# The w_out sums and parts on VectorE and ScalarE, in 44 held steps

## The chip, the cores and the metric

The kernel runs on one core of a Trainium2 chip. The metric is the device time of one execution in microseconds (us). Engines are named as in the profile: PE is TensorE, DVE VectorE, ACT ScalarE, POOL GpSimd; SP is the engine that issues the DMAs.

## The reference

One step of a streaming encoder layer: 4096 prompt frames and 64 sample frames of width 1024. A projection feeds two groups of heads with gated linear recurrences, each branch has a SiLU gate, and an output projection closes the layer. What matters here is the end:

```python
    o_a = rms_norm(o_a, g_on_gla).reshape(B, T, GLA_V) * jax.nn.silu(z_a)
    o_h = rms_norm(o_h, g_on_hgrn).reshape(B, T, HGRN_W) * jax.nn.silu(z_h)
    o = jnp.einsum('bte,ed->btd', jnp.concatenate([o_a, o_h], axis=-1), w_out)
    y = x + gate[:, None] * rms_norm(o, g_post)
```

`z_h` is the last of the input projections; the line with `z_h` is the gate part, the einsum with `w_out` the output product.

## The kernel before

The program runs in stages: setup and first group, the GLA projections and recurrence in 16 groups of 256 frames, the HGRN projections and recurrence in 16 groups, the gate part, and the output product. All float32 products are made from two parts: a high part `hi` (a cast to the matmul's format, on ScalarE) and a low part `lo` (source minus `hi`). Three matmuls, hi by hi, hi by lo, lo by hi, make one product. The helper `split` (L87 to L94) makes both parts: the cast is L93, the subtraction L94, on VectorE unless another engine is handed in.

**The gate part** is `zrun` in `run`. It goes through 33 tiles: two of 128 frames for each of the 16 groups, and the 64 sample frames as a third tile of group 2. For each group, `split_h` makes the parts `hh` of the normalised input in four pieces (casts on ScalarE, subtractions on VectorE), `hh` has five buffers, and `load_hf` starts the loads of the next group's input. `z_tile` (L1240 to L1256) loads one tile of `oh`, makes 24 matmuls of 128x512 (eight k, three products each, L624), a sigmoid on ScalarE (L1252), two products on VectorE (L1253, L1254) and stores the tile. A tile gives three yields: after half of its matmuls, at its end, and once in `zrun`.

**The output product** (`project`) multiplies two-by-two blocks with seven products in place of eight. It needs seven weight forms per k tile: B11, B21, B22 as they are, and the sums T1 to T4. **`load_wout`** (L1267) makes them from `w_out`: in each of four rounds (`kt`) it loads two pieces of 128x1024 (L1284) into the two buffers of the staging pool, scales each by a column of norm gains on ScalarE (L1285), makes four sums in place (L1290) and splits seven blocks of 128x512 into hi and lo (`put`). A staging buffer is loaded again for the next round when its last reader is done. The seven results go to the rooms `wv`, `wb` and `wc`.

**The order.** `weave(main, sides)` runs a main generator and, between its steps, so many steps of each side generator. The tuple `(generator, n, first, last)` spreads n side steps evenly over the main steps from `first` to `last`. What comes out is a program order. A scheduler then orders each engine's queue by simulated readiness, so an instruction whose inputs are ready early may go ahead of others traced before it; the engine itself takes its queue in order. `keep_in_program_order(ins)` ties an instruction behind the one traced just before it on the same engine: an edge of issue order only, which does not wait for that instruction to finish. Instructions traced later are not tied by it.

The last tiles of the gate part are run after the weave, the last one inside `project`. The gate part from tile 8 to tile 29 is the main of the weave at L1672: 22 tiles, 66 main steps. Its only side is `load_wout`, in 16 steps over main steps 0 to 56.

Of the kernel before, what the change touches and what calls it, by code (L numbers as in the profile page):

```python
# [6 lines left out]
F32 = mybir.dt.float32  # L7
# [3 lines left out]
AF = mybir.ActivationFunctionType  # L11
ALU = mybir.AluOpType
# [16 lines left out]
class Kernel:  # L29
# [1108 lines left out]
    def attend_group(self, g, S, Ss, res, G, NS, scratch, out_p, out_s):  # L1138
# [4 lines left out]
        def run(i):  # L1143
# [28 lines left out]
            )  # L1172

        main = run(0)
        if len(sets) == 1:
            yield from main
        else:

            sample = run(1)
            level = None  # L1180
            for _ in main:
                if level is not LEVELS:
                    level = next(sample)
                    if level is LEVELS:
                        nc.sync.dma_start(self.s_room, self.state_ap(Ss[0], G, NS))
                        Ss[0] = self.s_room
                yield
            assert level is LEVELS
            yield from sample
            nc.sync.dma_start(self.state_ap(out_s, G, NS), Ss[0])  # L1190
# [76 lines left out]
    def load_wout(self, room):  # L1267

        nc = self.nc
        W = self.W3  # L1270
        names = ("B11", "B21", "B22", "T1", "T2", "T3", "T4")
        for n in names:
            W[n] = []
        rooms = [("wv", i) for i in range(8)] + [("wb", i) for i in range(8)]

        def unit():
            u = self.wunit(rooms.pop(0)[0]) if rooms else room.tile([P, 1024], F32R, name="wc", bufs=12)
            return u[:, :1024].rearrange("p (two c) -> p two c", two=2)

        def load(kt):  # L1280
            sts = []
            for q in range(2):
                st = self.stage_pair()[:, :D]
                nc.sync.dma_start(st, self.t["w_out"][0, (4 * q + kt) * P : (4 * q + kt + 1) * P, :])  # L1284
                nc.scalar.activation(st, st, AF.Copy, scale=self.col[:, 50 + q : 51 + q])  # L1285
                sts += [st[:, :512], st[:, 512:]]
            return sts

        def sub(dst, a, b):
            nc.gpsimd.tensor_tensor(dst, a, b, ALU.subtract)  # L1290

        for kt in range(4):
            b11, b12, b21, b22 = load(kt)
            yield
            us = {n: unit() for n in names}

            def put(n, src):
                self.split(us[n][:, 0], us[n][:, 1], src, nc.gpsimd)


            put("B11", b11)
            sub(b11, b12, b11)
            sub(b12, b22, b12)
            yield
            put("B22", b22)
            put("B21", b21)
            sub(b22, b22, b11)
            sub(b21, b21, b22)
            yield
            for n, src in (("T1", b11), ("T3", b12), ("T2", b22), ("T4", b21)):  # L1310
                put(n, src)
            for n in names:
                W[n].append(us[n])
            yield
# [267 lines left out]
    def run(self):  # L1582
        nc, t = self.nc, self.t
        self.W1 = W1 = {"qk": [], "z": [], "v": []}
        self.W2 = W2 = {"q": [], "f": [], "i": []}
        self.W3 = W3 = {"z": [], "o": []}

        def now(gen):
            for _ in gen:
                pass  # L1590

        self.setup()
        ng = self.ng
        with ExitStack() as rec:
            self.open_recurrence(rec)
            self.setup_late()
            for i in range(4):
                nc.sync.dma_start(self.h_d[0][:, 2 * i : 2 * i + 2, :], self.hf[i])
            h = lambda k: self.h0[k // 2][:, :, k % 2]
            S, Ss = [None], [t["state_gla"]]  # L1600
            side = None

            def prep_x(g):
                if g > 1:
                    self.x_load(g, [0, 1])
                (self.x_norm if g < 2 else self.quad_norm)(g, [0, 1])
                for _ in range(3):
                    yield
                yield from self.x_turn(g)

            def prep_h(g, tl):
                self.load_hf(g, tl)
                yield

            for g in range(ng):
                prep = prep_x(g + 1) if g + 1 < ng else prep_h(0, self.groups2[0])
                sides = [(side, 12, 1, 18), (prep, 8, 0, 16) if g == 0 else (prep, 8, 7, 19)]
                if g == ng - 1:

                    sides.append((self.weights(W2["f"], C_FH, 512, "wa"), 10, 8, 18))  # L1620
                    sides.append((self.weights(W2["q"], C_QH, 512, "wv"), 10, 20, 26))
                res = self.weave(self.proj_gla(g, h), sides)
                h = self.split_h()
                side = self.attend_group(g, S, Ss, res, 2, 2, self.oa_d, t["new_gla_p"], t["new_gla_s"])
                next(side)
            S, Ss = [None], [t["state_hgrn"]]
            gate = self.gate_rows()
            per_gate = -(-28 // max(1, ng - self.beside - 2))
            for g in range(ng):
                prep = prep_h(g + 1, self.groups2[g + 1]) if g + 1 < ng else prep_h(0, self.groups2[0])  # L1630
                sides = [
                    (side, 15 if g == 0 else 16 if g == self.beside + 1 else 12, 1, 18), (prep, 1, 4, 8),
                    (gate if g > self.beside + 1 else None, per_gate, 0, END),
                ]
                if g == 0:
                    sides.append((self.weights(W2["i"], C_IH, 512, "wb"), 10, 0, 14))
                if g == ng - 1:
                    sides.append((self.weights(W3["z"], C_ZH, 512, "wa"), 10, 8, 18))
                res = self.weave(self.proj_hgrn(g, h), sides)
                h = self.split_h()  # L1640
                side = self.attend_group(g, S, Ss, res, 4, 1, self.oh_d, t["new_hgrn_p"], t["new_hgrn_s"])
                next(side)
            now(gate)
            tiles = [(g, j, tl) for g in range(ng) for j, tl in enumerate(self.groups2[g])]
            self.done = 0

            def zrun():
                hh = h
                for i, (g, j, tl) in enumerate(tiles):
                    if j == 0 and i > 0:  # L1650
                        hh = self.split_h()
                        if len(self.groups2[g]) == 3:
                            self.pair_up(hh, [self.stage_pair(F32R)])
                    if j == 0 and g + 1 < ng:
                        self.load_hf(g + 1, self.groups2[g + 1])
                    yield from self.z_tile(hh, tiles[i])
                    self.done += 1
                    yield

            zg = zrun()  # L1660

            def until(n):
                while self.done < n:
                    next(zg)
                    yield

            self.weave(until(8), [(side, 15, 0, 22)])
        self.x_room.close()
        with ExitStack() as s:
            room = self.pool(s, "w3", reuse_waits="tile")  # L1670
            self.ogp = self.pool(s, "og", reuse_waits="tile")
            self.weave(until(len(tiles) - 3), [(self.load_wout(room), 16, 0, 56)])  # L1672
            ogs = [self.og_half(0, j, q, self.ep if j else None) for j in range(2) for q in range(2)]
            now(until(len(tiles) - 1))
            self.project(ogs, lambda: now(zg))
# [58 lines left out]
```

## Time and profile before

| what | value |
|---|---|
| time, median of 3 runs | 2133.59 us (2131.57 to 2134.98) |
| the profiled execution's own time | 2135.26 us |
| its span, first to last instruction | 2133.4 us |
| granted TensorE clock, mean | 0.991 |

The page's second part cuts the span into 40 slices of 53 us; the gate part lies in slices 29 to 33, counted from 0. The digits are busy tenths.

```profile
DVE  6877776777767778687888788777786446777775
ACT  5666655666555655445444444444444434333432
POOL 3200011000010111110000001100125502232321
PEclk9999999999999999999999999999999899999999
```

GpSimd's two fives are slices 30 and 31, the one 8 of the clock is slice 31, VectorE's two fours are slices 31 and 32.

In the rows that follow, a timeline row has the start, the duration, the engine, the line, the operation, out<-in, shape and count, and in brackets the idle time ahead of it and what ended it. Matmuls are pipelined, so a row's duration is a merged one and its end is modelled. DMA waits are put down to the transfer that landed last.

### The profile page before, as it was taken

The numbers are of one execution on the slowest core, as the hardware profiler recorded it, in microseconds if no ns is written. First come the engines' busy times: TensorE is split into PE (matmuls) and PEld (weight loads), VectorE is DVE, ScalarE is ACT, GpSimd is POOL, SyncE is SP. The second block draws the span as 40 slices with busy tenths as digits, with TensorE's granted clock in tenths as the row PEclk, the third lists the DMA queues.
The fourth block names the chain that finished last, engine by engine and source line by source line (L and its number), as shares of the span: only waits on it lengthen the run. The fifth ranks groups of instructions, "written<-read, shape, count | busy, mean of one in ns | idle before, by whom it ended". The sixth has DMA issues, their size and how long they took to land.

```text
span 2133.4 us, 45130 instructions
## 1 busy us (share of the span) xinstructions
PE 2073.7 (97%) x16390; PEld 1817.6 (85%) x16390; DVE 1563.9 (73%) x4742; ACT 1061.4 (50%) x3124; POOL 376.2 (18%) x745
## 2 busy tenths in 40 slices
PE   7999999999999999999999999999999799999998
PEld 5888898988988888989988989999876688888886
DVE  6877776777767778687888788777786446777775
ACT  5666655666555655445444444444444434333432
POOL 3200011000010111110000001100125502232321
PEclk9999999999999999999999999999999899999999
DMA  8422222222222331011111101110245565354442
GB/s 253 122 56 73 67 59 53 55 67 67 58 56 51 104 114 43 31 36 58 50 51 60 52 31 36 31 31 31 75 149 179 171 197 163 131 166 138 158 143 95
DMA packets 236106, 190.00 MB, mean 89 GB/s; under 512 B 138220, under 2 KB 160208, under 8 KB 235884
## 3 DMA queue, kind: packets, MB, share of 16 engines
q1 hardware_dynamic: 235740, 186.86, 29.5%
q8 instruction: 129, 2.11, 0.4%
q14 instruction: 93, 0.76, 0.1%
q10 hardware_dynamic: 144, 0.26, 0.0%
HBM read 126.60 MB, written 60.45 MB: 88 GB/s over the span
## 4 chain that ended last, share of the span: by engine, by line
PE 80%; DVE 9%; ACT 4%; POOL 2%; DMA 2%; issue 2%; SPq 1%; DVEq 0%; ACTq 0%; POOLq 0%
PE ps_pj L624 28%; PE ps_pj L612 21%; PE ps_pj L1336 12%; PE ps_ms L844 2%; PE ps_o L828 2%; PE ps_o L823 2%; PE ps_o L1336 2%; PE ps_at L691 2%; PE ps_at L963 2%; DVE wst L914 2%; PE ps_at L771 1%; PE ps_tp L798 1%; POOL wst L1290 1%; DMA wst<-in_w_in_dram 1%; ACT A L781 1%
## 5 line engine op out<-in xcount | busy, mean ns | idle before, releaser
L612 PE MATMUL ps_pj<-hh,wa 128*128 128x256 f32 (+1 forms) x2976 | 392.1, 287 | 0.0
L624 PE MATMUL ps_pj<-wb,hh 128*128 128x512 f32 x1536 | 378.8, 396 | 0.9 <-ACT K L1043 0.9
L612 PEld LDWEIGHTS ps_pj<-hh,wa 128*128 128x128 f32 x2976 | 372.7, 191 | 4.9 <-issue 0.3
L624 PEld LDWEIGHTS ps_pj<-wb,hh 128*128 128x128 f32 x1536 | 280.3, 188 | 59.1 <-issue 2.7
L612 PE MATMUL ps_pj<-hh,wv 128*128 128x256 f32 (+1 forms) x1536 | 213.2, 289 | 0.0
L624 PE MATMUL ps_pj<-wa,hh 128*128 128x512 f32 x768 | 190.1, 406 | 16.1 <-ACT hh L93 8.7
L612 PEld LDWEIGHTS ps_pj<-hh,wv 128*128 128x128 f32 x1536 | 191.8, 188 | 12.1 <-issue 9.3
L624 PE MATMUL ps_pj<-wv,hh 128*128 128x264 f32 x1464 | 199.3, 290 | 1.6 <-DVE wv L94 1.6
L624 PEld LDWEIGHTS ps_pj<-wa,hh 128*128 128x128 f32 x768 | 147.2, 195 | 53.9 <-ACT hh L93 11.8
L624 PEld LDWEIGHTS ps_pj<-wv,hh 128*128 128x128 f32 x1464 | 184.1, 188 | 6.8 <-issue 2.3
L945 POOL COPY T<-T 128x16 f32<-128x16 f32 (+1 forms) x32 | 9.9, 310 | 1007.6 <-DVE Qg L884 904.3
L94 DVE TENSOR_TENSOR hh<-hf,hh 128x512 fp32r<-128x512 f32 (+1 forms) x188 | 140.5, 756 | 41.9 <-ACT hh L93 40.9
L1208 ACT ACTIVATE g<-ps_pj 128x256 f32<-128x256 f32 (+1 forms) x128 | 49.6, 387 | 228.2 <-PE ps_pj L612 227.6
L93 ACT CAST hh<-hf 128x512 fp32r<-128x512 f32 (+1 forms) x188 | 116.9, 624 | 68.6 <-PE ps_pj L624 52.8
L914 DVE TENSOR_TENSOR wst<-wst,T 128x160 f32<-128x160 f32 (+4 forms) x480 | 108.5, 266 | 1.1
L1396 ACT ACTIVATE sq<-e 128x512 bf16<-128x512 f32 x64 | 40.4, 631 | 119.1 <-DVE e L1408 116.1
L1336 PE MATMUL ps_pj<-wc,wa 128*128 128x512 f32 x384 | 98.3, 391 | 0.0
L1399 POOL TENSOR_TENSOR e<-e,gg 128x512 f32<-128x512 f32 x32 | 41.4, 1293 | 294.5 <-ACT sq L1396 178.5
L938 ACT ACTIVATE A<-Ac,member 128x128 f32<-128x128 f32 x256 | 80.8, 390 | 24.4 <-DVE Ac L932 24.4
L947 POOL TENSOR_TENSOR T<-T,T 128x16 f32<-128x16 f32 (+1 forms) x224 | 83.8, 374 | 17.0
L1336 PEld LDWEIGHTS ps_pj<-wc,wa 128*128 128x128 f32 x384 | 72.0, 188 | 16.0
L932 DVE COPY_PREDICATED Ac<-mask,ps_at 128x112 f32<-128x112 uint8 (+6 forms) x448 | 77.4, 224 | 1.0 <-PE ps_at L963 0.9
(337 smaller groups left out, 4082.2 us busy)
## 6 DMA issues: line engine op xcount, KB each, us to landing
hf<-h_d SPq DMA_DIRECT2D x128, 256.0 KB
h_d<-hf SPq DMA_DIRECT2D x64, 256.0 KB
oh_d<-e SPq DMA_DIRECT2D x64, 256.0 KB
xq<-in_x_prompt_dram SPq DMA_DIRECT2D x64, 256.0 KB
out_y_prompt_dram<-xq SPq DMA_DIRECT2D x63, 256.0 KB
xt<-in_x_prompt_dram SPq DMA_DIRECT2D x448, 32.0 KB
wst<-in_w_in_dram SPq DMA_DIRECT2D x36, 256.0 KB
e<-oh_d SPq DMA_DIRECT2D x33, 256.0 KB
```

The lines of the kernel that those rows point to most:

```text
L93: self.nc.scalar.copy(hi, src)
L94: (eng or self.nc.vector).tensor_tensor(lo, src, hi.bitcast(F32), ALU.subtract)
L612: self.nc.tensor.matmul(ps[:, :T], a, b, start=i == 0, stop=i == n - 1)
L624: self.nc.tensor.matmul(ps[:r, : c1 - c0], a, b, start=kt == 0 and i == 0, stop=kt == KT - 1 and i == 2)
L691: nc.tensor.transpose(pt[:, i * P : (i + 1) * P], D[:, c + i, :], self.ident)
L823: nc.tensor.matmul(po[h], A[:, c * 4 + h, :], v, start=h < n, stop=St is None and h == 4 - n)
L914: nc.vector.tensor_tensor(parts(dst), parts(src), t.unsqueeze(3).to_broadcast(shape), ALU.mult)
L932: nc.vector.copy_predicated(Ach[:, :, 4 * a :].rearrange("p h (j m) -> p h j m", m=4), self.mask[:CL, : 8 - a].unsqueeze(1).unsqueeze(3).t ...
L938: nc.scalar.activation(Ah[:, :, 32 * b : 32 * b + 32], Ach, AF.Copy, scale=self.member[:CL, 8 + b : 9 + b])
L947: nc.gpsimd.tensor_tensor(E8[:, :, i], E8[:, :, i - 1], T8[:, :, i], ALU.mult)
L1208: nc.scalar.activation(sg, pf[:, :T], AF.Sigmoid)
L1336: nc.tensor.matmul(bank, u[:, a, kt, :], W[name][kt][:, b], start=kt + i == 0, stop=kt + i == 5)
```

## The change

`load_wout` is rewritten in its order and its engines. The four sums (`sub`) and the low parts (in `put`) are computed by VectorE where GpSimd computed them. Loads and scalings are separated: the scalings follow two yields after the loads, with a yield after each. Each round has 11 yields where it had four, with at most one `put` and one sum between two of them; the seven puts come in another order. Each scaling, cast, sum and low part is tied by `keep_in_program_order`; the loads are not. The weave spreads 44 steps over main steps 0 to 62.

```diff
+        here = self.tc.keep_in_program_order
+
+        def sub(dst, a, b):
+            here(nc.vector.tensor_tensor(dst, a, b, ALU.subtract))
+
         def load(kt):
             sts = []
             for q in range(2):
                 st = self.stage_pair()[:, :D]
                 nc.sync.dma_start(st, self.t["w_out"][0, (4 * q + kt) * P : (4 * q + kt + 1) * P, :])
-                nc.scalar.activation(st, st, AF.Copy, scale=self.col[:, 50 + q : 51 + q])
-                sts += [st[:, :512], st[:, 512:]]
+                sts.append(st)
             return sts
 
-        def sub(dst, a, b):
-            nc.gpsimd.tensor_tensor(dst, a, b, ALU.subtract)
-
         for kt in range(4):
-            b11, b12, b21, b22 = load(kt)
-            yield
+            sts = load(kt)
+            yield
+            yield
+            for q, st in enumerate(sts):
+                here(nc.scalar.activation(st, st, AF.Copy, scale=self.col[:, 50 + q : 51 + q]))
+                yield
+            b11, b12, b21, b22 = [st[:, o : o + 512] for st in sts for o in (0, 512)]
             us = {n: unit() for n in names}
 
             def put(n, src):
-                self.split(us[n][:, 0], us[n][:, 1], src, nc.gpsimd)
+                here(nc.scalar.copy(us[n][:, 0], src))
+                sub(us[n][:, 1], src, us[n][:, 0].bitcast(F32))
 
 
             put("B11", b11)
+            yield
             sub(b11, b12, b11)
+            put("B22", b22)
+            yield
             sub(b12, b22, b12)
-            yield
-            put("B22", b22)
+            put("T1", b11)
+            yield
+            sub(b22, b22, b11)
+            put("T3", b12)
+            yield
             put("B21", b21)
-            sub(b22, b22, b11)
+            yield
             sub(b21, b21, b22)
-            yield
-            for n, src in (("T1", b11), ("T3", b12), ("T2", b22), ("T4", b21)):
-                put(n, src)
+            put("T2", b22)
+            yield
+            put("T4", b21)
             for n in names:
                 W[n].append(us[n])
             yield
...
-            self.weave(until(len(tiles) - 3), [(self.load_wout(room), 16, 0, 56)])
+            self.weave(until(len(tiles) - 3), [(self.load_wout(room), 44, 0, 62)])
```

## The prediction

> **What bounds the kernel now.** I read the page first, then the same views cut down to the stage that the change touches. The page gives one row for TensorE as a whole and one for the gate part's matmuls (out<-in, shape, count, busy us, mean ns, then the idle time ahead of them and what ended it).
>
> ```profile
> PE 2073.7 (97%) x16390; PEld 1817.6 (85%) x16390; DVE 1563.9 (73%) x4742; ACT 1061.4 (50%) x3124; POOL 376.2 (18%) x745
> L624 PE MATMUL ps_pj<-wa,hh 128*128 128x512 f32 x768 | 190.1, 406 | 16.1 <-ACT hh L93 8.7
> ```
>
> TensorE is busy 97% of the span, so only its idle time and its slow time can be won. The gate matmuls have 16.1 us of idle ahead of them, more than half of it ended by the cast of the next `hh` on ScalarE. Cutting the stage into stretches shows where (busy us and counts by engine, granted clock, DMA):
>
> ```profile
> core 0: us, PE busy (x) PEld busy (x) DVE busy (x) ACT busy (x) POOL busy (x), PEclk, DMA share, GB/s
> 1561.00:1606.50 45.50, 45.50 (x326) 35.24 (x325) 40.77 (x128) 23.06 (x58) 10.78 (x26) 1.00 0.52 165
> ...
> 1615.00:1636.00 21.00, 19.08 (x74) 14.32 (x72) 11.92 (x11) 9.17 (x16) 14.87 (x11) 0.92 0.52 175
> 1636.00:1650.00 14.00, 11.32 (x46) 8.40 (x46) 8.95 (x8) 6.22 (x12) 12.51 (x8) 1.00 0.43 136
> 1650.00:1670.00 20.00, 13.64 (x44) 9.60 (x44) 7.78 (x8) 7.96 (x14) 14.87 (x11) 0.77 0.49 165
> 1670.00:1688.60 18.60, 13.51 (x48) 10.22 (x48) 9.11 (x10) 11.21 (x19) 15.47 (x11) 0.87 0.50 157
> 1688.60:1770.00 81.40, 81.38 (x353) 67.22 (x354) 39.94 (x60) 24.52 (x41) 0.00 (x0) 0.98 0.60 191
> ```
>
> From 1615 to 1688.6 GpSimd is busy three quarters of the time, and TensorE has gaps and a granted clock down to 0.77. From 1688.6, when GpSimd has nothing left, TensorE has no gap. In order of time, TensorE's rows are:
>
> ```profile
> 1606.52 13.77 PE L624 MATMUL ps_pj<-wa,hh 128*128 128x512 f32 x60
> 1620.79 0.73 PE L624 MATMUL ps_pj<-wa,hh 128*128 128x512 f32 x2 [0.50 <-ACT hh L93]
> 1622.65 13.11 PE L624 MATMUL ps_pj<-wa,hh 128*128 128x512 f32 x48 [1.13 <-DVE hh L94]
> 1636.49 10.16 PE L624 MATMUL ps_pj<-wa,hh 128*128 128x512 f32 x42 [0.73 <-DVE hh L94]
> 1647.50 1.20 PE L624 MATMUL ps_pj<-wa,hh 128*128 128x512 f32 x4 [0.85 <-DVE hh L94]
> 1650.31 2.80 PE L624 MATMUL ps_pj<-wa,hh 128*128 128x512 f32 x6 [1.61 <-ACT hh L93]
> 1654.03 10.11 PE L624 MATMUL ps_pj<-wa,hh 128*128 128x512 f32 x36 [0.91 <-ACT hh L93]
> 1667.18 0.73 PE L624 MATMUL ps_pj<-wa,hh 128*128 128x512 f32 x2 [3.04 <-ACT hh L93]
> 1670.20 12.78 PE L624 MATMUL ps_pj<-wa,hh 128*128 128x512 f32 x46 [2.30 <-DVE hh L94]
> 1685.59 0.73 PE L624 MATMUL ps_pj<-wa,hh 128*128 128x512 f32 x2 [2.60 <-ACT hh L93]
> 1688.62 81.50 PE L624 MATMUL ps_pj<-wa,hh 128*128 128x512 f32 x352 [2.30 <-DVE hh L94]
> ```
>
> These rows hold 600 matmuls, which is 25 tiles of 24 (eight k, three products each), and take 1606.52 to 1770.12 = 163.6 us. Every gap waits for `hh`. Why `hh` is late stands in the chain that ended last, followed through 1600 to 1790, and in the table of waits of 1586 to 1712 (us in total, times, longest):
>
> ```profile
> by line: PE ps_pj L624 49.6%; POOL wst L1290 9.9%; DMA wst<-in_w_out_dram 6.9%; POOL wb L94 6.3%; PE ps_pj L1336 5.8%; POOL wc L94 4.5%; issue 4.0%; DVE hh L94 2.7%; PE ps_pj L632 1.9%; POOL wv L94 1.6%; PE ps_at L1327 0.9%; ACT hh L93 0.7%
> ACT wst L1285 <- DMA wst<-in_w_out_dram: 12.1, 5, 4.5
> ACT wc L93 <- POOL wst L1290: 12.3, 6, 3.3
> ACT wst L1285 <- POOL wb L94: 4.3, 1, 4.3
> ```
>
> The chain runs through the w_out work itself: 22.3% of these 190 us on GpSimd, 6.9% on the w_out loads. ScalarE takes its instructions in order; a cast of a w_out part that waits for a GpSimd subtraction holds up the `hh` cast queued behind it, and TensorE starves.
>
> **The change part by part.** The costs of one instruction, from the groups of the same window (busy us, mean ns):
>
> ```profile
> L94 DVE TENSOR_TENSOR hh<-hf,hh 128x512 fp32r<-128x512 f32 x33 | 33.7, 1030 | 18.8 <-ACT hh L93 18.7
> L1290 POOL TENSOR_TENSOR wst<-wst 128x512 f32<-128x512 f32 x16 | 23.3, 1459 | 17.7 <-ACT wst L1285 17.1
> L1285 ACT ACTIVATE wst<-wst,col 128x1024 f32<-128x1024 f32 x8 | 9.2, 1148 | 19.6 <-DMA wst<-in_w_out_dram 12.1 <-POOL wb L94 4.3 <-POOL wv L94 3.2
> ```
>
> And how the same stage looks without w_out work, first on ScalarE, then on VectorE:
>
> ```profile
> 1704.88 0.60 ACT L1252 ACTIVATE e<-ps_pj 128x512 f32<-128x512 f32 x1 [4.33 <-PE ps_pj L624]
> 1706.28 0.62 ACT L93 CAST hh<-hf 128x512 fp32r<-128x512 f32 x1 [0.81 <-PE ps_pj L624]
> ...
> 1710.32 0.60 ACT L1252 ACTIVATE e<-ps_pj 128x512 f32<-128x512 f32 x1 [0.74 <-DVE hh L94]
> ```
>
> ```profile
> 1706.94 0.69 DVE L94 TENSOR_TENSOR hh<-hf,hh 128x512 fp32r<-128x512 f32 x1
> ...
> 1710.95 0.69 DVE L1253 TENSOR_TENSOR e<-ps_pj,e 128x512 f32<-128x512 f32 x1 [0.64 <-ACT e L1252]
> 1711.56 0.68 DVE L94 TENSOR_TENSOR hh<-hf,hh 128x512 fp32r<-128x512 f32 x1
> ```
>
> *Removed.* Sigmoid to sigmoid (1704.88, 1710.32) a full-speed tile takes 5.44 us, 227 ns a matmul. 25 tiles would take 136.0 us; the stage loses 163.6 - 136.0 = 27.6 us. It splits into idle, the ten bracketed gaps: 16.0 us; and clock: 0.08 x 21 + 0.23 x 20 + 0.13 x 18.6 + 0.02 x 81.4 = 10.3 us; 1.3 us is left at the edges. So each us of gap has cost 1.64 us. I take the clock loss to go with the gaps: the granted clock is 1.00 in the stretch before, with no idle, and below 0.98 only where gaps are.
>
> [...]
>
> *Moved to VectorE.* Each of the four rounds has 4 sums and 7 low parts, 44 subtractions in all; they go from GpSimd (1459 ns for the sums) to VectorE. There the same shape takes 0.69 us when GpSimd is quiet (the row at 1706.94) and 1.03 us on average while GpSimd works. Issue to issue it is 0.61 us (1710.95 to 1711.56). 44 x 0.69 = 30.4 us, spread over 62 of the 66 steps of the 22 tiles, that is 20.7 tiles or 112 us. VectorE is 39.94/81.40 = 49% busy in the quiet stretch; it becomes 49 + 27 = 76%. The stretch 1561 to 1606.5 ran at 40.77/45.50 = 90% on VectorE without a TensorE gap. The second tile of a pair is the tightest: two products of its own, three `hh` low parts, up to four of the new ones, 9 x 0.65 (between the two figures) = 5.9 us in 5.44. A backlog of half a us meets a slack of 4.0: the second `hh` part is done at 1707.63 (1706.94 + 0.69), and TensorE wants it six matmuls (1.4 us) into the next tile, which follows at 1770.12 - 11 x 5.44 = 1710.3, so at 1711.7. Cost: nothing, with VectorE's spare quarter as cover.
>
> *Kept on ScalarE.* 8 scalings of 1.15 us and 28 casts of 0.62 are the same as before, 26.6 us, now over 112 us: 30% (24.52/81.40) + 24% = 54%. Cost nothing. What disappears is the wait inside: a cast now waits for a VectorE subtraction of 0.69 us issued a step earlier.
>
> *The pacing.* A step of the side work now comes every 62/44 = 1.41 main steps, 2.6 us (a main step is 5.44/3 = 1.81). No step has more than two VectorE and two ScalarE instructions.
>
> *The held order.* Each held instruction is tied to the one traced before it on its engine. Later `hh` casts are not tied, so they can still go ahead, as the cast at 1706.28 goes ahead of its own tile's sigmoid at 1710.32. The added wait is the scaling's for its w_out load; queued behind it on ScalarE are `hh` casts and sigmoids. The load-to-scaling time, from two rows:
>
> ```profile
> 1627.03 0.38 SPq L1284 DMA_DIRECT2D wst<-in_w_out_dram  x1
> ...
> 1633.31 1.15 ACT L1285 ACTIVATE wst<-wst,col 128x1024 f32<-128x1024 f32 x1 [4.47 <-DMA wst<-in_w_out_dram]
> ```
>
> That is 6.3 us, the slowest; now two steps (5.1 us) lie between. A wait of 1.2 us, under the 4.0 us of slack. The loads are not held; the first half's buffer comes free at the T3 part, four steps before the scaling's round begins, so mostly there is no wait. The SP queue has eight loads as before; each waits for VectorE instead of GpSimd, and the `hf` loads behind it have a tile and more to spare.
>
> *Tail.* The last step falls at main step 62, tile 28 to 29 of 33; the products need the weights after tile 32, over 15 us later. Nothing is bought or lost.
>
> *Sum.* Gaps 16.0, of which I leave 1.0 for bunched steps, and clock 10.3: 25.3 us. The profiled execution took 2135.26 us: 2135.3 - 25.3 = 2110.0. It was 1.7 us above the median of the runs shown, so **2108.3** beside that median.
>
> **The rivals.**
>
> 1. *A new wait takes the place.* If SP issues the loads of a round only when the scaling's turn has come, ScalarE stands for the whole 6.3 us once a round: 2.3 more than the slack, times 1.64, times 4 rounds = 15 us given back: 2123. For: the loads share SP with stores that wait for VectorE, and 12.1 us went to this wait before. Against: a round has 11 x 2.6 = 28 us, and its chain needs about 6.3 + 2.3 + 7 x 0.62 + 0.69 = 14.
>
> 2. *The clock stays low.* If the slow clock comes of something other than the gaps, only the gaps go, 15 us: 2118.6. For: no single gap fills the spell of slow clock behind it. Against: the clock column. [...]
>
> 3. *No change.* The w_out chain itself stays the bound, with VectorE in GpSimd's place: 2133.6. Against: the chain's 40 us of GpSimd shrink by half and are spread.
>
> 4. *Slower: the `hh` casts lose their lead.* If the held instructions in effect fence the queue, the casts of a pair come only after the sigmoid that ends the pair before. Place: each of the 11 pairs of the stretch. Price: 0.60 sigmoid, 1.15 scaling, 0.62 cast, 0.69 low part, 3.1 us of gap, 5.0 with the clock, 55 us in all against the 27.6 removed: about 2161. It decides from 27.6/11/1.64 = 1.5 us a pair. Against: the tie binds one instruction to its forerunner, and the `hh` casts carry none.
>
> **How the numbers follow.** Forecast (2104 to 2114: all 27.6 and a little from the stage before, or gaps of 3 us left) 0.73; rival 1 0.13; rival 2 0.02; rival 3 0.04; rival 4 0.08. About 0.2% (4 us) is what a measurement here can tell from no change. Faster 0.73 + 0.13 + 0.02 = 0.88, same 0.04, slower 0.08. The range reaches from the forecast's low end over rival 2 to milder forms of rival 1 (gaps of half its size, 2116, to nearly all of it), 2104 to 2122; rivals 3 and 4 and the fullest form of rival 1 lie outside, some 0.15.
>
> **What would show it.** Right: no GpSimd rows in the gate part; no bracketed gap over 1 us ahead of L624 between 1606 and 1745; a granted clock of 0.98 or more throughout; VectorE at 70 to 80% there, its `hh` low parts at 0.69 us instead of 1.03; 25 tiles in about 138 us. Wrong: gaps ahead of L624 ended by ScalarE with scalings waiting for loads (rival 1), clock under 0.9 without gaps (2), or a gap of 2 us or more at each pair's start (4). The prediction also fails if stages outside 1561 to 1770 move by more than 3 us, since nothing there is edited.

## The result and the profile after

| | before | after |
|---|---|---|
| time, median | 2134.19 us (4 runs, 2131.57 to 2134.98) | 2106.08 us (4 runs, 2102.63 to 2107.43) |
| the profiled execution, time and span | 2135.26, 2133.4 us | 2102.63, 2100.9 us |
| gate stage, 600 matmuls from the first after the sample tile to the first transpose of the output product | 163.4 us | 136.0 us |

The ratio is 0.9868, 95% interval 0.9851 to 0.9885: 28 us faster, between 24 and 32. The forecast was 2108.3.

The stage is where the time came from. TensorE's rows of after, in order of time, over the part that had eleven rows and ten gaps before:

```profile
1601.92 136.17 PE L624 MATMUL ps_pj<-wa,hh 128*128 128x512 f32 x600
1737.92 0.60 PE L1341 MATMUL ps_tp<-ident,e 128*128 128x128 f32 x4
```

One row, 600 matmuls, no gap: 136.0 us, which is 25 tiles at the 5.44 us that the quiet tiles took before. The stretches of after (busy us and counts by engine, granted clock, DMA):

```profile
core 0: us, PE busy (x) PEld busy (x) DVE busy (x) ACT busy (x) POOL busy (x), PEclk, DMA share, GB/s
...
1615.00:1636.00 21.00, 21.00 (x95) 17.38 (x94) 15.83 (x26) 11.56 (x21) 0.00 (x0) 1.00 0.61 203
1636.00:1650.00 14.00, 14.00 (x64) 11.58 (x63) 8.11 (x13) 6.45 (x10) 0.00 (x0) 1.00 0.80 260
1650.00:1670.00 20.00, 20.00 (x90) 16.57 (x89) 16.02 (x26) 11.19 (x19) 0.00 (x0) 1.00 0.65 204
1670.00:1688.60 18.60, 18.60 (x84) 15.40 (x83) 12.75 (x21) 9.55 (x16) 0.00 (x0) 1.00 0.65 226
```

The granted clock is 1.00 in the four stretches where it went down to 0.77, and GpSimd is empty. The chain that ended last, from 1600 to 1760, had 22.3% on GpSimd; in after it is TensorE:

```profile
by line: PE ps_pj L624 88.4%; PE ps_pj L1350 6.9%; PE ps_pj L632 1.4%; PE ps_o L1350 1.3%; PE ps_at L1341 1.1%; PE ps_tp L1341 0.5%; PE ps_ms L1341 0.5%
```

The groups of 1586 to 1745 (busy us, mean ns, idle ahead) show the moved work and the `hh` low parts beside it:

```profile
L94 DVE TENSOR_TENSOR hh<-hf,hh 128x512 fp32r<-128x512 f32 x52 | 34.9, 686 | 8.2 <-ACT hh L93 7.8
...
L1284 DVE TENSOR_TENSOR wst<-wst 128x512 f32<-128x512 f32 x16 | 10.9, 683 | 0.0
L1299 ACT ACTIVATE wst<-wst,col 128x1024 f32<-128x1024 f32 x8 | 9.0, 1144 | 0.0
```

The scalings (L1299) wait for nothing; they had 19.6 us of idle ahead of them. The `hh` low parts take 0.69 us where they took 1.03.

The two profiled spans differ by 32.5 us, of which 27.4 are the stage. Another 4.6 lie ahead of it, in unchanged code (the sample tile's matmuls start at 1598.15 instead of 1602.76). In the first 60 us of the span the granted clock was 0.91 in this execution of before and 0.97 in that of after. Of the 4.6 us, 4.1 are there by the first matmul of the sample frames (731.6 instead of 735.7). Over all profiled kernels the start of the stage lies anywhere from 1601.9 to 1608.2, whatever the edit, so it is scatter between executions, most of it from the start of the program, and the stage's length is the better measure of an edit. It is used below; each length is that of one profiled execution.

### The profile page after: what moved, and what is told of

Same layout as the page of the kernel before. It is cut to its first block, busy times and chain, and to the rows that moved or that the text cites. A ratio compares the mean times of both kernels' runs of the same rounds, so it can differ in the third digit from the quotient of the medians.

```text
span 2100.9 us, 45104 instructions
## 1 busy us (share of the span) xinstructions
PE 2060.6 (98%) x16390; PEld 1813.0 (86%) x16390; DVE 1572.4 (75%) x4786; ACT 1061.7 (51%) x3124; POOL 313.6 (15%) x701
## 4 chain that ended last, share of the span: by engine, by line
PE 85%; DVE 9%; ACT 4%; issue 1%; DMA 1%; SPq 0%; DVEq 0%; POOL 0%; ACTq 0%; POOLq 0%
PE ps_pj L624 31%; PE ps_pj L612 22%; PE ps_pj L1350 12%; PE ps_ms L844 2%; PE ps_o L828 2%; PE ps_o L823 2%; PE ps_o L1350 2%; PE ps_at L691 2%; PE ps_at L963 2%; DVE wst L914 2%; PE ps_at L771 1%; PE ps_tp L798 1%; ACT A L781 1%; PE ps_at L1341 1%; PE ps_pj L632 1%
## 5 line engine op out<-in xcount | busy, mean ns | idle before, releaser
L624 PE MATMUL ps_pj<-wa,hh 128*128 128x512 f32 x768 | 178.8, 392 | 0.0
L94 DVE TENSOR_TENSOR hh<-hf,hh 128x512 fp32r<-128x512 f32 (+1 forms) x188 | 128.4, 694 | 24.9 <-ACT hh L93 23.5
L855 DVE SCALAR_TENSOR_TENSOR S<-S,T,ps_ms 128x128 f32<-128x128 f32 x186 | 54.3, 341 | 32.3 <-PE ps_ms L844 32.1
```

What stands on the lines that cost most here:

```text
L94: (eng or self.nc.vector).tensor_tensor(lo, src, hi.bitcast(F32), ALU.subtract)
L624: self.nc.tensor.matmul(ps[:r, : c1 - c0], a, b, start=kt == 0 and i == 0, stop=kt == KT - 1 and i == 2)
L855: nc.vector.scalar_tensor_tensor(Sn[:, g, :], St[:, g, :], T[:, c * G + g, 0:1], pd[:, g, :], ALU.mult, ALU.add)
```

## The experiments

The change does three things: the engine of the subtractions, the ties, the finer steps. Six of the twelve kernels fill the table of all combinations; the others test prices that the prediction named. "Free" means without the ties, and each ratio is to the runs of before that were taken beside that kernel. "ScalarE waits" is what its w_out instructions waited for sums, earlier readers and loads, summed from the table of waits from 1585 to 1738 or 1745.

| engine, ties, steps | stage us | ScalarE waits us | median us | ratio to before |
|---|---|---|---|---|
| GpSimd, free, 16 (before) | 163.4 | 39.1 | 2134.19 | |
| GpSimd, free, 44 | 161.1 | 39.4 | 2132.08 | 0.9989 (0.9978 to 1.0000) |
| GpSimd, tied, 16 | 141.5 | 10.6 | 2109.90 | 0.9884 (0.9852 to 0.9916) |
| GpSimd, tied, 44 | 136.1 | 11.8 | 2107.00 | 0.9881 (0.9861 to 0.9900) |
| VectorE, free, 16 | 136.4 | 21.0 | 2106.44 | 0.9877 (0.9862 to 0.9891) |
| VectorE, free, 44 | 138.4 | 21.8 | 2107.65 | 0.9885 (0.9868 to 0.9901) |
| VectorE, tied, 16 | 136.0 | 5.4 | 2103.66 | 0.9865 (0.9845 to 0.9885) |
| VectorE, tied, 44 (after) | 136.0 | 6.3 | 2106.08 | 0.9868 (0.9851 to 0.9885) |

**The engine alone.** Before, with two words changed:

```diff
-            nc.gpsimd.tensor_tensor(dst, a, b, ALU.subtract)
+            nc.vector.tensor_tensor(dst, a, b, ALU.subtract)
...
-                self.split(us[n][:, 0], us[n][:, 1], src, nc.gpsimd)
+                self.split(us[n][:, 0], us[n][:, 1], src)
```

> Stage length here is from the gate part's first 128x512 matmul after the sample tile to the first transpose of the output product: 163.4 us in before (1606.52 to 1769.96), 136.0 us in after (1601.92 to 1737.92). This kernel is before with the sums and low parts on VectorE, order and 16 steps as they were. If waiting for GpSimd was the cause, the waits for L1290 and for the w_out low parts shrink with the instruction (0.69 us for 1.46) and the stage takes 140 us or less, about 2110 us in all. If the order was the cause (instructions that go ahead and then wait for loads, in bursts), gaps ended by the hh cast stay, the stage takes 150 us or more and the time is 2119 us or more.

The stage took 136.4 us, with no gap. The loads were waited for as before (from the waits of 1600 to 1740: total, times, longest), so waits for loads did not by themselves starve TensorE:

```profile
ACT wst L1285 <- DMA wst<-in_w_out_dram: 13.3, 5, 6.0
...
ACT wc L93 <- DVE wst L1290: 4.0, 3, 2.4
```

What fell is the wait for sums, 12.3 us to 4.0 for the casts into `wc`. That speaks for GpSimd as the cause. The next run speaks against it.

**GpSimd, tied and fine.** After with GpSimd's subtractions back:

```diff
-            here(nc.vector.tensor_tensor(dst, a, b, ALU.subtract))
+            here(nc.gpsimd.tensor_tensor(dst, a, b, ALU.subtract))
```

> After with the sums and low parts back on GpSimd, held and in 44 steps. If GpSimd's slowness was the cause, the casts still wait for it (44 x 1.4 = 62 us of GpSimd in 112 us, VectorE's hh low parts back near 1.0 us) and the stage takes 150 us or more. If the order was the cause, the stage stays under 141 us.

It missed the first theory: 136.1 us and no gap, though GpSimd's instructions are longer than before (1604 ns a sum for 1459) and VectorE is slower beside them (1177 ns for an `hh` low part, 686 in after):

```profile
1605.32 136.31 PE L624 MATMUL ps_pj<-wa,hh 128*128 128x512 f32 x600
```

```profile
L94 DVE TENSOR_TENSOR hh<-hf,hh 128x512 fp32r<-128x512 f32 x48 | 55.2, 1177 | 9.4 <-ACT hh L93 9.2
...
L1284 POOL TENSOR_TENSOR wst<-wst 128x512 f32<-128x512 f32 x16 | 25.7, 1604 | 0.6
```

So at this pace neither a slow GpSimd nor a VectorE slowed by it costs TensorE anything.

**VectorE without ties, and VectorE tied in the old steps.** After without its ties, and the old 16 steps with VectorE and ties:

```diff
-        here = self.tc.keep_in_program_order
+        here = lambda ins: ins
```

> After without the ties: same engines, same 44 steps, the scheduler may send the instructions ahead. If the engine is what mattered, the stage stays within 3 us of 136 and the time within 4 us of after. If the ties matter, casts and scalings go ahead of the hh casts and wait for loads again: gaps ended by the hh cast, a stage of 145 us or more.

138.4 us, with one gap of 1.29 us ended by an `hh` cast. With VectorE the ties are not needed, though loads are waited for 15.0 us without them. The second kernel is the one of the first experiment with `here(...)` around the scalings, casts, sums and low parts:

> VectorE and ties, but the old order and the old 16 steps. The largest step has four casts and four low parts, 2.5 us of ScalarE and 2.8 of VectorE, under the 4.0 us of slack: if slack decides, the stage stays under 139 us. The scaling now follows its load without a step between; if that wait decides (up to 6.3 us, four rounds), the stage takes 148 us or more with gaps behind scalings that wait for loads.

136.0 us, no gap: the finer steps are not needed either. ScalarE waited 5.4 us for loads, 3.0 at most.

**GpSimd without ties, in fine steps.** The kernel of the second experiment with the `lambda` above:

> After with GpSimd and without ties: only the 44 finer steps and their order are left of the change. Stage length as in the runs before this one (before 163.4 us, after 136.0, and 136 to 138 with any of VectorE alone, ties alone, or VectorE without ties). If the loss needs GpSimd and the freedom to go ahead together, and the steps do little, the stage takes 150 us or more. If finer steps are the third thing that is enough by itself, it stays under 141 us.

The "ties alone" of this text is the second experiment, which has ties and fine steps. The stage took 161.1 us, and the median shows no gain that is clear of the noise (the interval of the ratio ends at 1.0000). The gaps are back, and so is the cause, in TensorE's rows and in the waits:

```profile
1685.10 1.22 PE L624 MATMUL ps_pj<-wa,hh 128*128 128x512 f32 x2 [6.84 <-ACT hh L93]
```

```profile
ACT wc L1305 <- POOL wst L1284: 16.8, 6, 6.5
...
ACT wst L1299 <- DMA wst<-in_w_out_dram: 10.5, 4, 5.0
```

**GpSimd, tied, in the old steps.** Before with `here(...)` around the four kinds of instruction and nothing else:

> Before with ties only: GpSimd, the old order, 16 steps. If the ties alone are enough, the stage stays under 141 us. If what counts is how long ScalarE stands in one go, the step of four puts decides: its casts wait behind GpSimd sums of 1.3 to 1.6 us, and the next scaling waits for its load (up to 6 us) with no step between, more than the 4.0 us of slack: gaps in each round, a stage of 145 us or more.

It fell between: 141.5 us. One gap of 2.41 and one of 0.51 us stay, and from 1654 to 1658, behind the first, the granted clock is 0.58 and 0.57.

```profile
1605.17 45.50 PE L624 MATMUL ps_pj<-wa,hh 128*128 128x512 f32 x200
1653.08 46.41 PE L624 MATMUL ps_pj<-wa,hh 128*128 128x512 f32 x196 [2.41 <-DVE hh L94]
1700.01 46.78 PE L624 MATMUL ps_pj<-wa,hh 128*128 128x512 f32 x204 [0.51 <-ACT hh L93]
```

So ties win 22 of the 27 us by themselves, VectorE wins all, and the finer steps show only with GpSimd and ties (141.5 to 136.1); in the medians that last difference, 2109.90 to 2107.00 with two runs each, is not clear of the noise. Among these eight kernels the loss needs GpSimd and freedom together.

What the ties change is the pace. Here is the first scaling of the second round and of the fourth, in before and then in the tied, fine kernel with GpSimd:

```profile
1625.47 1.15 ACT L1285 ACTIVATE wst<-wst,col 128x1024 f32<-128x1024 f32 x1 [3.22 <-POOL wv L94]
...
1670.14 1.15 ACT L1285 ACTIVATE wst<-wst,col 128x1024 f32<-128x1024 f32 x1 [3.02 <-DMA wst<-in_w_out_dram]
```

```profile
1644.09 1.15 ACT L1299 ACTIVATE wst<-wst,col 128x1024 f32<-128x1024 f32 x1
...
1703.93 2.18 ACT L1299 ACTIVATE wst<-wst,col 128x1024 f32<-128x1024 f32 x2
```

Two rounds take 44.7 us in before and 59.8 us tied; they take 41.0 us with GpSimd, free, in fine steps and 52.8 us with GpSimd, tied, in the old ones. The low parts of the last round end 40 us later than in before. With VectorE and no ties two rounds take only 35.6 us (old steps) and 32.7 us (fine steps), and TensorE loses 0.4 and 2.4 us: a fast pace is harmful where the subtractions are slow.

**The pace alone.** GpSimd tied and fine, but the steps put over 36 main steps (65 us) for 62; and the same with VectorE:

```diff
-            self.weave(until(len(tiles) - 3), [(self.load_wout(room), 44, 0, 62)])
+            self.weave(until(len(tiles) - 3), [(self.load_wout(room), 44, 0, 36)])
```

> The held and fine kernel with GpSimd (stage 136.1 us over 62 main steps) with its 44 steps over main steps 0 to 36, 65 us. Without ties the w_out work ran as fast as its own chain allowed, about 80 us for four rounds, and the stage was lost; with ties it was spread over about 110 us. If the pace is what the ties give, GpSimd (70 us of work) cannot keep 65 us, ScalarE stands behind it again, and the stage takes 150 us or more. If the place in the queue is what counts (each cast behind the work of its own tile), the stage stays under 143 us.

156.6 us, and 2125.91 us in all (ratio 0.9963, 0.9947 to 0.9979): three quarters of the loss come back with the ties in place. Two rounds take 44.3 us, nearly the pace of before:

```profile
1634.97 1.14 ACT L1299 ACTIVATE wst<-wst,col 128x1024 f32<-128x1024 f32 x1
...
1679.26 1.14 ACT L1299 ACTIVATE wst<-wst,col 128x1024 f32<-128x1024 f32 x1
```

ScalarE's w_out instructions wait 39.7 us again, as in the two kernels without ties (39.1 and 39.4):

```profile
1642.40 1.20 PE L624 MATMUL ps_pj<-wa,hh 128*128 128x512 f32 x2 [3.60 <-ACT hh L93]
...
1686.40 0.88 PE L624 MATMUL ps_pj<-wa,hh 128*128 128x512 f32 x2 [3.48 <-ACT hh L93]
```

```profile
ACT wc L1305 <- POOL wst L1284: 14.7, 7, 4.4
...
ACT wst L1299 <- DMA wst<-in_w_out_dram: 10.0, 3, 4.1
...
ACT wb L1305 <- POOL wst L1284: 8.2, 4, 3.7
...
ACT wv L1305 <- POOL wst L1284: 6.8, 3, 4.5
```

So the spread is most of what the ties gave, and a tie by itself does not protect TensorE. The two free kernels with GpSimd took 4.5 and 6.8 us more than this one; whether that is the place in the queue was not tested. The same pace with VectorE:

> After with its 44 steps over main steps 0 to 36. VectorE then has 3.7 of the new subtractions a tile, 2.2 us beside 2.7 of its own in 5.4 us: 90%. If a VectorE queue with room is all that is needed, the stage stays within 3 us of 136; if the even spread is needed, gaps ended by hh low parts appear and the stage takes 140 us or more.

138.9 us (median 2107.65 us, ratio 0.9884, 0.9847 to 0.9922), at the edge of both: one gap of 2.46 us, ended by an `hh` low part. VectorE was busy 78% from 1613 to 1680, not 90%, so its mean load does not explain the gap. Two rows from just ahead of it:

```profile
1656.68 1.15 ACT L1299 ACTIVATE wst<-wst,col 128x1024 f32<-128x1024 f32 x1 [3.19 <-DMA wst<-in_w_out_dram]
```

```profile
1658.35 0.69 DVE L1253 TENSOR_TENSOR e<-ps_pj,e 128x512 f32<-128x512 f32 x1 [3.19 <-ACT e L1252]
```

A scaling stood 3.19 us for its load, the sigmoid queued behind it came late, and VectorE stood for the sigmoid. From 1659.68 on VectorE had no pause, and the `hh` low part that TensorE waited for came only at 1665.10, behind seven subtractions of the w_out work. That is the kind of wait that the prediction's first rival named, shorter than its 4.0 us of slack, and then a full VectorE queue. What the gap would be without the wait was not tested.

**VectorE's room.** After with each of the 28 low parts computed three times:

```diff
             here(nc.vector.tensor_tensor(dst, a, b, ALU.subtract))
+            for _ in range(2 if dst is not a and dst is not b else 0):
+                here(nc.vector.tensor_tensor(dst, a, b, ALU.subtract))
```

> After with each of the 28 low parts computed three times: 56 more VectorE instructions, 34 to 38 us in the same 112. If VectorE's spare quarter is the cover that the prediction named, VectorE passes 100% (76% and 31%), falls behind, and the stage takes 144 us or more, with gaps ahead of L624 ended by hh low parts. If VectorE's queue is not what covers it, the stage stays within 2 us of 136.

150.3 us and 2119.14 in all (0.9927, 0.9899 to 0.9956). The gaps are ended by VectorE, the largest near the end. VectorE did not reach 100% over the stretch: it was busy 92% from 1670 to 1742, and without a pause from 1732 to 1742:

```profile
1738.99 17.22 PE L624 MATMUL ps_pj<-wa,hh 128*128 128x512 f32 x68 [5.28 <-DVE hh L94]
```

So VectorE's room is a cover with an end: 44 subtractions in 112 us fit, 100 do not.

**The slower rival.** After with the `hh` casts and low parts of these tiles tied too:

```diff
-            self.split(u[:, 0], u[:, 1], self.hf[i])
+            if "T4" in self.W3 and len(self.W3["T4"]) < 4:
+                here = self.tc.keep_in_program_order
+                here(self.nc.scalar.copy(u[:, 0], self.hf[i]))
+                here(self.nc.vector.tensor_tensor(u[:, 1], self.hf[i], u[:, 0].bitcast(F32), ALU.subtract))
+            else:
+                self.split(u[:, 0], u[:, 1], self.hf[i])
```

> After with the hh casts and hh low parts of these tiles tied too, so that they cannot lead: the slower rival of the prediction, made on purpose. By its price a gap of 3.1 us and 1.64 us for each us of it at each of 11 pairs: 55 us, a stage near 190 us and about 2161 us. If the buffers of hh and the queue of tiles ahead cover a late cast, the stage stays under 145 us.

2143.67 us, slower than before (ratio 1.0042, 1.0026 to 1.0058); the stage takes 175.7 us. The mechanism is as the rival had it: a gap at the start of each pair, ten pairs, 26.0 us in all, and 39.7 us with the clock, in place of 55. Two of the pairs:

```profile
1708.43 1.21 PE L629 MATMUL ps_pj<-wa,hh 128*128 128x512 f32 x4 [1.71 <-ACT hh L592]
1710.67 10.27 PE L629 MATMUL ps_pj<-wa,hh 128*128 128x512 f32 x44 [1.02 <-DVE hh L593]
1722.64 1.21 PE L629 MATMUL ps_pj<-wa,hh 128*128 128x512 f32 x4 [1.71 <-ACT hh L592]
1724.88 10.28 PE L629 MATMUL ps_pj<-wa,hh 128*128 128x512 f32 x44 [1.02 <-DVE hh L593]
```

**Waits for loads.** After with each scaling traced right behind its load:

```diff
             sts = load(kt)
-            yield
-            yield
...
-            self.weave(until(len(tiles) - 3), [(self.load_wout(room), 44, 0, 62)])
+            self.weave(until(len(tiles) - 3), [(self.load_wout(room), 36, 0, 62)])
```

> After with each scaling traced right behind its load, without the two steps between (36 steps over the same 62): the first rival of the prediction, made on purpose. By its price ScalarE stands for the 6.3 us of a load once a round, 2.3 us over the slack, 1.64 us each, 15 us in all: a stage near 151 us. If a wait for a load falls into time in which ScalarE is idle anyway (it was 52% idle, and a wait of 6.0 us with VectorE and no ties left no gap), the stage stays under 139 us.

136.0 us (median 2105.27 us, ratio 0.9867, 0.9815 to 0.9918). The scalings waited 4.8 us for loads in three waits, 2.2 us the longest. The full 6.3 us did not arise, so this kernel does not test the rival's price. The first experiment had a wait of 6.0 us without a gap.

**More work for ScalarE.** After with the second scaling of each round repeated with a factor of 1.0:

```diff
                 here(nc.scalar.activation(st, st, AF.Copy, scale=self.col[:, 50 + q : 51 + q]))
+                for _ in range(2 * (kt + 1) if q else 0):
+                    here(nc.scalar.activation(st, st, AF.Copy, scale=1.0))
```

> After with extra work for ScalarE behind the second scaling of each round: it is repeated with a factor of 1.0, 2, 4, 6 and 8 times in the four rounds, 1.15 us each, to measure how long ScalarE may be taken before TensorE starves. By the prediction's slack of 4.0 us: no gap in rounds one and two (2.3 and 4.6 us less what lies between), 2 to 3 us in round three (6.9), 4 to 5 us in round four (9.2), and 1.64 us for each us of gap: a stage of 146 to 149 us. If the slack is a whole tile or more (5.4 us), only round four leaves gaps and the stage takes 143 us or less.

There are 20 more activations, 21.2 us, and the stage takes 136.1 us without a gap (median 2103.80 us, ratio 0.9860, 0.9827 to 0.9892). The first theory missed; the second has the bound right, but not the gaps of round four. ScalarE's rows in round three show why:

```profile
1675.16 1.06 ACT L1301 ACTIVATE wst<-wst 128x1024 f32<-128x1024 f32 x1
1676.12 0.61 ACT L93 CAST hh<-hf 128x512 fp32r<-128x512 f32 x1
1676.63 1.06 ACT L1301 ACTIVATE wst<-wst 128x1024 f32<-128x1024 f32 x1
```

The scheduler puts the `hh` casts between the repeated scalings. The longest piece of added work is 4.34 us, four in a row in round two, and it left no gap; so this kernel does not show how long ScalarE may be held before TensorE starves. It shows that 21 us of added work, spread by the scheduler, do not starve TensorE.

## Why the prediction was right

**The bound and the place.** Right. The loss was in the stretch 1615 to 1688.6, and all of it came back. One sign of failure that the prediction named did appear: the code ahead of the stage moved by more than 3 us, by 4.6. That code is not edited, and the start of the stage moves by up to 6.3 us among the profiled kernels, so the sign was set too tight for two single executions. "Gaps 16.0, of which I leave 1.0" and "1.3 us is left at the edges" were a little careful: nothing was left, so the stage gave 27.4 us where the sum had 25.3, and the median came 28.1 us lower, 2.2 below the forecast.

**Clock and gaps.** Right: the clock loss went with the gaps (1.00 in the whole stage). The rival with the clock staying low is out.

**Moved to VectorE.** Right in effect: no gap, `hh` low parts at 0.69 us. The step had VectorE at 76%; in the 112 us from 1613 to 1725 it is 72%:

```profile
1613.00:1725.00 112.00, 112.00 (x495) 92.72 (x494) 80.76 (x127) 59.30 (x98) 0.00 (x0) 1.00 0.68 221
```

ScalarE is at 53% (59.30 of 112), 54% was forecast.

**The mechanism.** Half right. "A cast of a w_out part that waits for a GpSimd subtraction holds up the `hh` cast queued behind it" is what the gaps of before show. ScalarE's rows about the longest of them, in which TensorE stood from 1664.14 to 1667.18:

```profile
1663.04 0.62 ACT L93 CAST wc<-wst 128x512 fp32r<-128x512 f32 x1 [3.14 <-POOL wst L1290]
1665.50 0.62 ACT L93 CAST wc<-wst 128x512 fp32r<-128x512 f32 x1 [1.84 <-POOL wst L1290]
1666.03 0.59 ACT L1252 ACTIVATE e<-ps_pj 128x512 f32<-128x512 f32 x1
1666.52 0.61 ACT L93 CAST hh<-hf 128x512 fp32r<-128x512 f32 x1
```

The matmuls that the sigmoid reads had ended by 1664.14, but ScalarE stood until 1665.50 for the cast ahead of it; the sigmoid began at 1666.03 and the `hh` cast that TensorE waited for at 1666.52. ScalarE kept to the order of its queue here. And the loss goes when GpSimd leaves. But the prediction put all of the gain on the engine and none on the pacing, which it costed only as harmless. The runs show that either is enough: with GpSimd kept, ties and fine steps give 136.1 us, and with the steps closer together 20.6 of the 27.4 us are lost again. The gain of the whole change was right; its division among the parts was not stated.

**The price of a gap,** 1.64 us for each us, held only as a mean: (150.3 - 136.0)/9.2 = 1.6 with the low parts tripled, 39.7/26.0 = 1.5 with `hh` tied, and 1.7 in both further kernels with GpSimd and many gaps (25.1/14.6 free in fine steps, 20.6/11.8 tied at the fast pace). With one or two gaps it was (141.5 - 136.0)/2.9 = 1.9 with GpSimd tied in 16 steps, 2.4/1.29 = 1.9 with VectorE free in fine steps, and 2.9/2.5 = 1.2 at the fast pace with VectorE.

**The held order.** Right: later `hh` casts are not tied and kept their lead. When they were tied too, the kernel became slower than before, as the fourth rival said, by 39.7 us of stage where it had 55: the gap came to 2.6 us a pair instead of 3.1, at ten pairs, and the price of a gap was lower.

**The slack of 4.0 us and the first rival.** The rival did not come about; in after the scalings wait for nothing. Its price was too high as far as the runs reach (a wait of 6.0 us without a gap, loads without lead and no gap), but no kernel had the full 6.3 us in each round, so the price stays open. So does the slack: 4.34 us of added work in one piece and the load wait of 6.0 us left no gap, while one of 3.19 us came ahead of a gap of 2.46. One figure for the whole stage does not describe it.

## What to carry to other kernels

When side work is woven into a stage that TensorE bounds, read the wait of the engine that both share: here 39 us of ScalarE waits in the side work went with 21 to 27 us lost on TensorE, and 22 us or less with 0 to 6. It is a sign and not a price: 10.6 us went with 5.5 and 21.0 with 0.4. It says nothing where the `hh` work itself is held: with `hh` tied the side work waited 4.7 us and the stage lost 39.7. Shortening the side work's own chain and spreading it evenly are two ways to the same end; one of them was enough here, and the simplest (two words) took nearly the whole gain (27.0 of 27.4 us of stage). A tie in the program order helped where it kept side work back, and made the slowest kernel of all where it held the work that must lead.

## What the runs showed of the hardware

Two gaps of nearly the same length were followed by different clocks. The kernel with GpSimd tied in 16 steps had one of 2.41 us, and the granted clock behind it was 0.58 and 0.57 over two stretches of 2 us (a loss of 0.42 and 0.43 in each us, or 1.7 us in all); the fast-paced kernel with VectorE had one of 2.46 us, and its granted clock stayed at 1.00. The stretches of the one, then of the other, from just before the gap on:

```profile
1650.00:1652.00 2.00, 0.67 (x3) 0.20 (x2) 2.00 (x2) 0.98 (x2) 2.00 (x2) 1.00 0.04 14
1652.00:1654.00 2.00, 0.92 (x4) 0.79 (x5) 2.00 (x2) 0.00 (x0) 2.00 (x2) 1.00 0.36 132
1654.00:1656.00 2.00, 2.00 (x7) 1.29 (x6) 2.00 (x2) 0.00 (x0) 1.92 (x3) 0.58 0.55 150
1656.00:1658.00 2.00, 2.00 (x6) 1.57 (x6) 2.00 (x3) 0.00 (x0) 1.54 (x1) 0.57 0.54 162
```

```profile
1664.00:1668.00 4.00, 2.16 (x9) 1.80 (x10) 4.00 (x7) 2.01 (x4) 0.00 (x0) 1.00 0.57 199
1668.00:1672.00 4.00, 4.00 (x19) 3.31 (x18) 3.12 (x6) 1.68 (x3) 0.00 (x0) 1.00 0.66 223
```

In before, gaps of only 0.50 and 1.13 us, with two matmuls between them, were followed by a granted clock of 0.50:

```profile
1624.00:1626.00 2.00, 2.00 (x7) 1.49 (x6) 2.00 (x4) 0.53 (x1) 1.43 (x1) 0.50 0.89 303
```

With `hh` tied, gaps of 1.71 and 1.02 us, with four matmuls between them, were not (1.00 from 1708 to 1722; the 44 matmuls behind them took 10.27 us). Why the clock fell behind some gaps and not behind others was not tested.
